# S5 prompt recurrence: a walk over chunk pairs, and a scan in levels in two halves

## The chip, the core and the metric

The kernel runs on one core of one Trainium2 chip. PE (TensorE) multiplies matrices, DVE (VectorE), ACT (ScalarE) and POOL (GpSimd) work on vectors, and SP issues most of the transfers. The metric is the device time of one execution in microseconds; lower is better. The profile is one execution of the same program, taken by the hardware profiler; its lines are explained where they are shown.

## The reference, cut to what matters

One layer of a decoder in float32: a prompt of 256 tokens and 8 samples of 4 tokens each. Two groups of heads run side by side on one input projection; the second, S5, is a diagonal complex recurrence over time.

```python
D_MODEL = 2048; SEQ = 256; DEC_BATCH = 8; DEC_SEQ = 4
S5_CH = 16; S5_GROUPS = 64; S5_STATE = 64

def s5_scan(u, lam_re, lam_im, log_step, b_re, b_im, c_re, c_im, d_skip, h0_re, h0_im):
    ...
    lam_bar = jnp.exp(lam * dt)
    ...
    bu = jnp.einsum('gpk,blgk->blgp', b_bar, uf.astype(jnp.complex64))
    h0 = lax.complex(h0_re.astype(f32), h0_im.astype(f32))
    bu = bu.at[:, 0].add(lam_bar * h0)
    a = jnp.broadcast_to(lam_bar, bu.shape)
    def combine(e1, e2):
        a1, b1 = e1
        a2, b2 = e2
        return a1 * a2, a2 * b1 + b2
    _, h = lax.associative_scan(combine, (a, bu), axis=1)
    y = jnp.real(jnp.einsum('gkp,blgp->blgk', cmat, h)) + d_skip.astype(f32) * uf
    h_last = h[:, -1]
    return y, jnp.real(h_last), jnp.imag(h_last)

def layer(x, c, gla_s, s5_re, s5_im, conv_s, w):
    ...
    h = modulate(rmsnorm(x, w['norm1']), sh1, sc1)
    proj = jnp.einsum('bld,de->ble', h, w['w_in'])
    q, k, v, g, a_lr, u = jnp.split(proj, cuts, axis=-1)
    ...
    o, gla_new = gla_chunked(q, k, v, log_a, gla_s)
    ...
    y5, re_new, im_new = s5_scan(u.reshape(bsz, l, S5_GROUPS, S5_CH), ...)
    ...
```

The layer goes on with a gated output projection, a convolution over three tokens and a feed-forward part; these are not touched.

## The kernel before

**Tiles and stages.** Every weight comes from HBM once, as tiles `raw` of 128x1024. ACT (line 126) makes the high part `wh` of one, DVE (line 128) the rest `wl`, and PE runs three matmuls for each block of 128 rows (lines 143 to 145: `wh` with the high part of the input, `wh` with its low part, `wl` with the high part). All 288 tokens, 32 of the samples and 256 of the prompt, lie side by side, so such a matmul is 128x288. Between the projections stand groups of matmuls of the condition vector (line 191, `ada`), which use a `raw` without a split.

**S5.** Four tokens make a chunk. The prompt has 64 chunks and the samples one each, so the state `st` has per partition 2 (real, imaginary) x 32 blocks of two channel groups x 73 columns: 8 for the samples' start states, one of zeros, 64 for the chunks. For each of the 8 projections f of u (lines 653 to 684), PE finishes the projection and transposes it twice (lines 663 and 669, with the tiles `us` and, copied by ACT, `vt`), and multiplies with the input matrices (line 679); ACT copies the result into four blocks of `st` and into `deci`, the samples' part (lines 680 and 681). A complex product of a coefficient and a state is done as two multiplies and two adds over both parts, the second with the parts swapped. `advance` (line 647) does that with `a4`, the transition over one chunk: after each f it adds every even chunk (0, 2, ...) to the odd one behind it, on POOL, for f=7 on DVE. With all eight f done, the samples' end state is made on DVE (lines 686 to 690) and written out by a transfer that POOL issues (line 691, `o_s5d`).

**The walk.** Then, on POOL, the loop of line 692 goes over the chunk pairs: 31 steps, each of which takes the state two chunks back, multiplies it with `a8` (the transition over two chunks) and adds it to the present one, for all 32 blocks at once, 128x64:

```python
for c in range(3, NC4, 2):
    ...
    G.tensor_tensor(q1, prev, a8[:, 0], op=ALU.mult)
    G.tensor_tensor(q2, prevs, a8[:, 1], op=ALU.mult)
    G.tensor_tensor(cur, cur, q1, op=ALU.add)
    G.tensor_tensor(cur, cur, q2, op=ALU.add)
```

The last column is the prompt's end state (line 703). Later, for each f (lines 841 to 868), `advance` fills the chunks between (31 columns, on DVE for even f, on POOL for odd), PE makes the outputs (line 853 from the input, line 855 from `st` with `cA`), ACT copies them to `zt`, and PE transposes back.

**What else runs there.** Projections m=8 to 15 (lines 707 to 713), the attention matrix of the other group in levels of 32, 16, 8, 4, 2 and 1 tokens (lines 763 to 781: two differences and two products on DVE, an exponential on ACT, then matmuls in line 738 or 752), its states (lines 785 to 833), and projections m=16 to 23 (lines 835 to 838). The first level's tile takes the slot `S11` that `deci` had, so it waits until `o_s5d` is read out.

**What sets the order.** Each engine works through its own list. A scheduler makes the lists from the program's order and its own estimate of durations; a rank far ahead is given only to the loading and splitting of weights (`high_priority`, lines 105, 114, 124), and the ada groups are kept in one piece (`chained`, line 165). The ring `t2k` has three buffers of 128x512 (line 236), which `vt`, `zt`, `dt1` and the products `q` of `advance` share in the order in which the program names them.

Of the kernel before, what the change touches and what calls it, by code (L numbers as in the profile page):

```python
# [12 lines left out]
F32 = mybir.dt.float32  # L13
# [3 lines left out]
ALU = mybir.AluOpType  # L17
# [3 lines left out]
P = 128  # L21
# [35 lines left out]
def tile_hybrid_step(ctx: ExitStack, tc: _tile.TileContext, a: dict):  # L57
# [15 lines left out]
    def nm(s):  # L73
        cnt[0] += 1
        return f"{s}_{cnt[0]}"
# [159 lines left out]
    with ExitStack() as early:  # L235
# [83 lines left out]
        V.tensor_sub(w1, w1, w2)  # L319
        V.tensor_mul(fi, w1, den)  # L320

        def bc16(x):
            return x.unsqueeze(2).to_broadcast([P, 32, 16])

# [296 lines left out]
        for h in range(H):  # L621
# [9 lines left out]
            V.tensor_sub(l2, l2, l1)  # L631
            V.tensor_tensor_scan(cum[:, h], cst[:, C_RST:C_RST + NT], l2, 0.0, op0=ALU.mult, op1=ALU.add)


        a4 = epb.tile([P, 2, 2, 32], F32, name="a4")
        a8 = epb.tile([P, 2, 2, 32], F32, name="a8")
        for t in (a4, a8):
            if t is a4:
                V.tensor_copy(t[:, 0, 0], AP[:, 3, 0])
                V.tensor_copy(t[:, 1, 1], AP[:, 3, 1])  # L640
            else:
                cmul(t[:, 0, 0], t[:, 1, 1], AP[:, 3, 0], AP[:, 3, 1], AP[:, 3, 0], AP[:, 3, 1],
                     t[:, 0, 1], t[:, 1, 0])
            V.tensor_copy(t[:, 0, 1], t[:, 0, 0])
            V.tensor_scalar_mul(t[:, 1, 0], t[:, 1, 1], -1.0)

        def advance(eng, dst, src, srcs, fs, n):
            for w_, x in ((0, src), (1, srcs)):
                q = t2k.tile([P, 512], F32, tag="t2k", name=nm("q"))[:, 0:8 * n].rearrange(
                    "p (r a c) -> p r a c", r=2, a=4)  # L650
                eng.tensor_tensor(q, x, a4[:, w_, :, fs].unsqueeze(3).to_broadcast([P, 2, 4, n]), op=ALU.mult)
                eng.tensor_tensor(dst, dst, q, op=ALU.add)

        ut = []
        for f in range(8):
            m = f
            ps = proj2(f)
            us = sml.tile([P, 4, NCOL], F32, tag="us", name=nm("us"))
            V.tensor_tensor(us, ps.rearrange("p (c s) -> p s c", s=4), pu[f].rearrange("p (c s) -> p s c", s=4),
                            op=ALU.add)  # L660
            pvv = ps_s5()
            for s in range(4):
                T.transpose(pvv[0:NCOL, s * P:(s + 1) * P], us[:, s], ident)
            vt = t2k.tile([P, 512], F32, tag="t2k", name=nm("vt"))
            S.copy(vt[0:NCOL].rearrange("p (g s k) -> p s g k", g=8, s=4),
                   pvv[0:NCOL].rearrange("p (s g k) -> p s g k", s=4, g=8))
            puu = ps_s5()
            for aj in range(4):
                T.transpose(puu[:, aj * NCOL:(aj + 1) * NCOL], vt[0:NCOL, aj * P:(aj + 1) * P], ident[0:NCOL, 0:NCOL])
            u_f = slot(f"UU{f}", [P, 4, NCOL])  # L670
            S.copy(u_f, puu[:, 0:4 * NCOL].rearrange("p (a c) -> p a c", a=4))
            ut.append(u_f)
            for r in range(2):
                pi = ps_gl()[:, 0:4 * NCOL].rearrange("p (a c) -> p a c", a=4)
                for al_ in range(4):
                    pr = 4 * f + al_
                    for j in range(2):
                        js = slice(64 * j, 64 * j + 64)
                        T.matmul(pi[js, al_], pt_t[pr // 16][r][js, pr % 16], u_f[js, al_], start=True, stop=True)
                S.copy(st[:, r, 4 * f:4 * f + 4, NB + 1:], pi[:, :, NB:])  # L680
                S.copy(deci[:, r, 4 * f:4 * f + 4], pi[:, :, 0:NB])
            fs = slice(4 * f, 4 * f + 4)
            advance(V if f == 7 else G, st[:, :, fs, NB + 2::2], st[:, :, fs, NB + 1::2], st[:, ::-1, fs, NB + 1::2], fs, 32)
            step(ada_b, 1)

        dt1 = t2k.tile([P, 512], F32, tag="t2k", name="dt1").rearrange("p (r a b) -> p r a b", r=2, a=32)
        for w_, src in ((0, st[:, :, :, 0:NB]), (1, st[:, ::-1, :, 0:NB])):
            for r in range(2):
                V.tensor_tensor(dt1[:, r], src[:, r], a4[:, w_, r].unsqueeze(2).to_broadcast([P, 32, NB]), op=ALU.mult)
            V.tensor_add(deci, deci, dt1)  # L690
        G.dma_start(a["o_s5d"], deci)
        for c in range(3, NC4, 2):
            prev = st[:, :, :, NB + c - 1]
            prevs = st[:, ::-1, :, NB + c - 1]
            cur = st[:, :, :, NB + c + 1]
            q1 = sml.tile([P, 2, 32], F32, tag="q1", bufs=1, name=nm("q1"))
            q2 = sml.tile([P, 2, 32], F32, tag="q2", bufs=1, name=nm("q2"))
            G.tensor_tensor(q1, prev, a8[:, 0], op=ALU.mult)  # L698
            G.tensor_tensor(q2, prevs, a8[:, 1], op=ALU.mult)  # L699
            G.tensor_tensor(cur, cur, q1, op=ALU.add)  # L700
            G.tensor_tensor(cur, cur, q2, op=ALU.add)  # L701
        s5p = epb.tile([P, 2, 32], F32, name="s5p")
        G.tensor_copy(s5p, st[:, :, :, NCOL])
        G.dma_start(a["o_s5p"], s5p)
# [135 lines left out]
        ybuf = []  # L840
        for f in range(8):
            fs = slice(4 * f, 4 * f + 4)
            advance(G if f % 2 else V, st[:, :, fs, NB + 3::2], st[:, :, fs, NB + 2:NCOL:2], st[:, ::-1, fs, NB + 2:NCOL:2],
                    fs, 31)
            zt = t2k.tile([P, 512], F32, tag="t2k", name=nm("zt"))
            ztv = zt[0:NCOL].rearrange("p (t a j k) -> p a j t k", t=4, a=4, j=2)
            pzs = [ps_s5()[0:NCOL, 0:256], ps_s5()[0:NCOL, 0:256]]
            for al_ in range(4):
                pr = 4 * f + al_
                for j in range(2):  # L850
                    js = slice(64 * j, 64 * j + 64)
                    o = pzs[j][:, al_ * 64:(al_ + 1) * 64]
                    T.matmul(o, ut[f][js, al_], mm_[js, pr], start=True, stop=False)  # L853
                    for r in range(2):
                        T.matmul(o, st[js, r, pr, 0:NCOL], cA[js, r, pr].rearrange("p t k -> p (t k)"),  # L855
                                 start=False, stop=(r == 1))
            for j in range(2):
                S.copy(ztv[:, :, j], pzs[j].rearrange("p (a t k) -> p a t k", a=4, t=4))
            py = ps_tr()
            for t_ in range(4):  # L860
                T.transpose(py[:, t_ * NCOL:(t_ + 1) * NCOL], zt[0:NCOL, t_ * P:(t_ + 1) * P], ident[0:NCOL, 0:NCOL])
            yb = slot(f"UU{f}", [P, NT])
            V.tensor_copy(yb.rearrange("p (c s) -> p s c", s=4),
                          py[:, 0:4 * NCOL].rearrange("p (s c) -> p s c", s=4))
            ybuf.append(yb)
            ps = proj2(24 + f)
            V.tensor_add(proj_dst(24 + f), ps, proj_dst(24 + f))
            step(ada_b, 1)
# [469 lines left out]
```

## Time and profile before

| | us |
|---|---|
| three runs | 1486.63, 1487.9, 1977.88 |
| their median | 1487.9 |
| the profiled execution | 1486.31 |
| its span in the profile | 1484.0 |
| mean granted clock of PE | 0.982 of full speed |

The span goes from the first to the last recorded instruction; some 2.3 us of the execution lie around it. The third run stands far above the other two, and the profiled execution is near the lower ones. Busy time of an engine is the sum of its instructions; matmuls overlap, so their number times their mean is more than PE's busy time.

### The profile page before, as it was taken

The numbers are of one execution on the slowest core, as the hardware profiler recorded it, in microseconds if no ns is written. First come the engines' busy times: TensorE is split into PE (matmuls) and PEld (weight loads), VectorE is DVE, ScalarE is ACT, GpSimd is POOL, SyncE is SP. The second block draws the span as 40 slices with busy tenths as digits, with TensorE's granted clock in tenths as the row PEclk, the third lists the DMA queues.
The fourth block names the chain that finished last, engine by engine and source line by source line (L and its number), as shares of the span: only waits on it lengthen the run. The fifth ranks groups of instructions, "written<-read, shape, count | busy, mean of one in ns | idle before, by whom it ended". The sixth has DMA issues, their size and how long they took to land.

```text
span 1484.0 us, 28963 instructions
## 1 busy us (share of the span) xinstructions
PE 1412.4 (95%) x11534; PEld 1301.3 (88%) x11534; DVE 903.6 (61%) x1646; ACT 681.2 (46%) x1142; POOL 347.9 (23%) x622
## 2 busy tenths in 40 slices
PE   4998999985999999899999999999999999999996
PEld 3877877874777898688999999999999999999995
DVE  7774673582366777755665666555656565566557
ACT  4741354333353446454435543454345534553445
POOL 1163013496211001322202220222023201330121
PEclk9999999997999999999999999999999999999998
DMA  9778978881689686678444435444544444445432
GB/s 374 278 287 233 383 278 287 282 299 70 241 286 335 244 311 234 248 265 289 168 175 170 163 141 191 161 170 157 171 169 159 171 160 167 166 161 170 147 104 79
DMA packets 88727, 316.95 MB, mean 214 GB/s; under 512 B 10368, under 2 KB 10784, under 8 KB 88592
## 3 DMA queue, kind: packets, MB, share of 16 engines
q1 hardware_dynamic: 84240, 299.72, 56.6%
q0 software_dynamic: 4064, 14.81, 2.9%
q8 instruction: 90, 1.47, 0.4%
q10 hardware_dynamic: 288, 0.59, 0.1%
q14 instruction: 45, 0.37, 0.1%
HBM read 306.63 MB, written 8.45 MB: 212 GB/s over the span
## 4 chain that ended last, share of the span: by engine, by line
PE 73%; POOL 4%; DVE 2%; DMA 1%; ACT 1%; issue 1%; DVEq 0%; SPq 0%; ACTq 0%; POOLq 0%
PE acc L143 22%; PE acc L145 22%; PE acc L144 22%; PE ada L191 3%; POOL q L699 1%; POOL st L701 1%; POOL q L698 1%; POOL st L700 1%; PE gl L918 1%; DMA raw<-wup 1%; PE s L855 1%; PE s L853 0%; DVE S L1071 0%; PE acc L1122 0%; PE gl L895 0%
## 5 line engine op out<-in xcount | busy, mean ns | idle before, releaser
L126 ACT CAST wh<-raw 128x1024 fp32r<-128x1024 f32 (+1 forms) x376 | 385.9, 1030 | 565.0 <-PE acc L144 486.4
L128 DVE TENSOR_TENSOR wl<-raw,wh 128x1024 fp32r<-128x1024 f32 (+1 forms) x376 | 454.6, 1211 | 297.6 <-ACT wh L126 287.3
L143 PE MATMUL acc<-hh,wh 128*128 128x288 f32 x1376 | 407.7, 296 | 0.0
L144 PE MATMUL acc<-hl,wh 128*128 128x288 f32 x1376 | 405.9, 295 | 0.0
L145 PE MATMUL acc<-hh,wl 128*128 128x288 f32 x1376 | 404.5, 294 | 0.0
L143 PEld LDWEIGHTS acc<-hh,wh 128*128 128x128 f32 x1376 | 257.8, 187 | 4.2 <-ACT up L1132 4.2
L145 PEld LDWEIGHTS acc<-hh,wl 128*128 128x128 f32 x1376 | 259.1, 188 | 0.0
L144 PEld LDWEIGHTS acc<-hl,wh 128*128 128x128 f32 x1376 | 258.3, 188 | 0.0
L1133 POOL COPY cvo<-up 128x16 f32<-128x16 f32 x88 | 101.7, 1156 | 595.5 <-ACT up L1131 595.5
L144 PE MATMUL acc<-ffhl,wh 128*128 128x288 f32 x704 | 208.1, 296 | 0.0
L145 PE MATMUL acc<-ffhl,wl 128*128 128x288 f32 x704 | 207.6, 295 | 0.0
L143 PE MATMUL acc<-ffhl,wh 128*128 128x288 f32 x704 | 207.1, 296 | 0.5 <-ACT ffhl L1163 0.2
L143 PE MATMUL acc<-h,wh 128*128 128x288 f32 x512 | 158.6, 311 | 4.3 <-ACT h L477 3.1
L145 PE MATMUL acc<-h,wl 128*128 128x288 f32 x512 | 153.7, 301 | 1.3 <-DVE wl L128 1.3
L144 PE MATMUL acc<-h,wh 128*128 128x288 f32 x512 | 153.7, 300 | 1.0 <-DVE h L478 1.0
L144 PEld LDWEIGHTS acc<-ffhl,wh 128*128 128x128 f32 x704 | 132.7, 188 | 0.1
L143 PEld LDWEIGHTS acc<-ffhl,wh 128*128 128x128 f32 x704 | 131.9, 188 | 0.9 <-ACT ffhl L1163 0.5
L145 PEld LDWEIGHTS acc<-ffhl,wl 128*128 128x128 f32 x704 | 132.0, 188 | 0.0
L1009 DVE SCALAR_TENSOR_TENSOR x<-acc,mod,x 128x256 f32<-128x256 f32 x128 | 61.6, 481 | 98.0 <-PE acc L145 97.7
L143 PEld LDWEIGHTS acc<-h,wh 128*128 128x128 f32 x512 | 97.7, 191 | 26.8 <-issue 9.4
L191 PE MATMUL ada<-raw,cS 128*32 128x512 f32 (+1 forms) x832 | 101.0, 574 | 5.8 <-DMA raw<-wadf 4.1
L145 PEld LDWEIGHTS acc<-h,wl 128*128 128x128 f32 x512 | 97.8, 191 | 2.0 <-DVE wl L128 1.5
(413 smaller groups left out, 1978.1 us busy)
## 6 DMA issues: line engine op xcount, KB each, us to landing
raw<-wup SPq DMA_DIRECT2D x176, 512.0 KB, 3.4
raw<-wadf SPq DMA_DIRECT2D x128, 512.0 KB, 6.1
raw<-wdn SPq DMA_DIRECT2D x80, 512.0 KB, 3.4
raw<-wadb SPq DMA_DIRECT2D x48, 512.0 KB, 7.8
raw<-win SPq DMA_DIRECT2D x32, 512.0 KB, 6.6
raw<-winc SPq DMA_DIRECT2D x32, 512.0 KB, 5.5
raw<-wout SPq DMA_DIRECT2D x32, 512.0 KB, 7.3
raw<-wad SPq DMA_DIRECT2D x16, 512.0 KB, 8.9
```

What stands on the lines that cost most here:

```text
L126: S.copy(wh, raw)
L128: V.tensor_sub(wl, raw, wh.bitcast(F32))
L143: T.matmul(ps, wh[:, ks], xh(k), start=first, stop=False)
L144: T.matmul(ps, wh[:, ks], xl(k), start=False, stop=False)
L145: tail[0] = T.matmul(ps, wl[:, ks], xh(k), start=False, stop=last).ins
L191: mms.append(lambda c=c, kc=kc_of(blk, j), raw=raw, c0=c0, first=first, last=last: T.matmul(ps[32 * c:32 * c + 32, 0:w], cS[:, kc, :], raw ...
L698: G.tensor_tensor(q1, prev, a8[:, 0], op=ALU.mult)
L699: G.tensor_tensor(q2, prevs, a8[:, 1], op=ALU.mult)
L700: G.tensor_tensor(cur, cur, q1, op=ALU.add)
L701: G.tensor_tensor(cur, cur, q2, op=ALU.add)
L1009: V.scalar_tensor_tensor(x2[:, m, ND:], ps[:, ND:], mod[:, vi, m, 0:1], x2[:, m, ND:], op0=ALU.mult, op1=ALU.add)
L1133: G.tensor_copy(cvo[:, m, 0:16].rearrange("p (b w) -> p b w", w=2), upd[:, :, 4:6])
```

## The change

The walk is replaced by `scan`, which works on 16 blocks at a time: after f=3 on blocks 0 to 15, after f=7 on blocks 16 to 31, both on POOL. After `advance` of level 0 (chunk pairs) it goes up: at level 1 every fourth chunk takes in the one two before it, at level 2 every eighth the one four before it, at level 3 every sixteenth the one eight before it. Then three steps one behind another carry the state over 16 chunks (level 4), and levels 3, 2 and 1 go down and fill the odd chunks between. Each advance is four instructions as before, so a half has 9 advances and 36 instructions, and the walk's 124 are gone. The coefficients are now powers of the transition over 1, 2, 4, 8 and 16 chunks (`apr`, `api`), made by DVE at the start of S5; `a4` and `a8` go. The products `q` of the scan come from the ring `t2k`, where the walk had its own `q1` and `q2`. The level-0 advances and those ahead of the outputs do the same arithmetic with the new tables.

```diff
--- before.py
+++ after.py
@@ -318,6 +318,21 @@
         V.tensor_mul(w2, w3, lam_i)
         V.tensor_sub(w1, w1, w2)
         V.tensor_mul(fi, w1, den)
+
+
+        apr = epb.tile([P, 5, 32], F32, name="apr")
+        api = epb.tile([P, 5, 2, 32], F32, name="api")
+        for i in range(5):
+            if i == 0:
+                V.tensor_copy(apr[:, 0], AP[:, 3, 0])
+                V.tensor_copy(api[:, 0, 1], AP[:, 3, 1])
+            else:
+                s_r, s_i = apr[:, i - 1], api[:, i - 1, 1]
+                cmul(apr[:, i], api[:, i, 1], s_r, s_i, s_r, s_i, w1, w2)
+            V.tensor_scalar_mul(api[:, i, 0], api[:, i, 1], -1.0)
+
+        def trans(w_, lev, fs):
+            return apr[:, lev, fs].unsqueeze(1).to_broadcast([P, 2, fs.stop - fs.start]) if w_ == 0 else api[:, lev, :, fs]
 
         def bc16(x):
             return x.unsqueeze(2).to_broadcast([P, 32, 16])
@@ -631,25 +646,29 @@
             V.tensor_sub(l2, l2, l1)
             V.tensor_tensor_scan(cum[:, h], cst[:, C_RST:C_RST + NT], l2, 0.0, op0=ALU.mult, op1=ALU.add)
 
-
-        a4 = epb.tile([P, 2, 2, 32], F32, name="a4")
-        a8 = epb.tile([P, 2, 2, 32], F32, name="a8")
-        for t in (a4, a8):
-            if t is a4:
-                V.tensor_copy(t[:, 0, 0], AP[:, 3, 0])
-                V.tensor_copy(t[:, 1, 1], AP[:, 3, 1])
-            else:
-                cmul(t[:, 0, 0], t[:, 1, 1], AP[:, 3, 0], AP[:, 3, 1], AP[:, 3, 0], AP[:, 3, 1],
-                     t[:, 0, 1], t[:, 1, 0])
-            V.tensor_copy(t[:, 0, 1], t[:, 0, 0])
-            V.tensor_scalar_mul(t[:, 1, 0], t[:, 1, 1], -1.0)
-
-        def advance(eng, dst, src, srcs, fs, n):
-            for w_, x in ((0, src), (1, srcs)):
-                q = t2k.tile([P, 512], F32, tag="t2k", name=nm("q"))[:, 0:8 * n].rearrange(
-                    "p (r a c) -> p r a c", r=2, a=4)
-                eng.tensor_tensor(q, x, a4[:, w_, :, fs].unsqueeze(3).to_broadcast([P, 2, 4, n]), op=ALU.mult)
+        def advance(eng, fs, lev, c0, dist, n):
+
+            na, back = fs.stop - fs.start, 1 << lev
+
+            def cols(rs, c):
+                return st[:, rs, fs, NB + 1 + c:NB + 2 + c + dist * (n - 1):dist]
+
+            dst = cols(slice(None), c0)
+            for w_, rs in ((0, slice(None)), (1, slice(None, None, -1))):
+                q = t2k.tile([P, 512], F32, tag="t2k", name=nm("q"))[:, 0:2 * na * n].rearrange(
+                    "p (r a c) -> p r a c", r=2, a=na)
+                eng.tensor_tensor(q, cols(rs, c0 - back), trans(w_, lev, fs).unsqueeze(3).to_broadcast([P, 2, na, n]),
+                                  op=ALU.mult)
                 eng.tensor_tensor(dst, dst, q, op=ALU.add)
+
+        def scan(eng, fs):
+
+            for lev in (1, 2, 3):
+                advance(eng, fs, lev, (2 << lev) - 1, 2 << lev, NC4 >> (lev + 1))
+            for c in range(31, NC4, 16):
+                advance(eng, fs, 4, c, 1, 1)
+            for lev in (3, 2, 1):
+                advance(eng, fs, lev, (3 << lev) - 1, 2 << lev, (NC4 >> (lev + 1)) - 1)
 
         ut = []
         for f in range(8):
@@ -680,25 +699,17 @@
                 S.copy(st[:, r, 4 * f:4 * f + 4, NB + 1:], pi[:, :, NB:])
                 S.copy(deci[:, r, 4 * f:4 * f + 4], pi[:, :, 0:NB])
             fs = slice(4 * f, 4 * f + 4)
-            advance(V if f == 7 else G, st[:, :, fs, NB + 2::2], st[:, :, fs, NB + 1::2], st[:, ::-1, fs, NB + 1::2], fs, 32)
+            advance(V if f == 7 else G, fs, 0, 1, 2, NC4 // 2)
+            if f % 4 == 3:
+                scan(G, slice(4 * f - 12, 4 * f + 4))
             step(ada_b, 1)
 
         dt1 = t2k.tile([P, 512], F32, tag="t2k", name="dt1").rearrange("p (r a b) -> p r a b", r=2, a=32)
         for w_, src in ((0, st[:, :, :, 0:NB]), (1, st[:, ::-1, :, 0:NB])):
             for r in range(2):
-                V.tensor_tensor(dt1[:, r], src[:, r], a4[:, w_, r].unsqueeze(2).to_broadcast([P, 32, NB]), op=ALU.mult)
+                V.tensor_tensor(dt1[:, r], src[:, r], (apr[:, 0] if w_ == 0 else api[:, 0, r]).unsqueeze(2).to_broadcast([P, 32, NB]), op=ALU.mult)
             V.tensor_add(deci, deci, dt1)
         G.dma_start(a["o_s5d"], deci)
-        for c in range(3, NC4, 2):
-            prev = st[:, :, :, NB + c - 1]
-            prevs = st[:, ::-1, :, NB + c - 1]
-            cur = st[:, :, :, NB + c + 1]
-            q1 = sml.tile([P, 2, 32], F32, tag="q1", bufs=1, name=nm("q1"))
-            q2 = sml.tile([P, 2, 32], F32, tag="q2", bufs=1, name=nm("q2"))
-            G.tensor_tensor(q1, prev, a8[:, 0], op=ALU.mult)
-            G.tensor_tensor(q2, prevs, a8[:, 1], op=ALU.mult)
-            G.tensor_tensor(cur, cur, q1, op=ALU.add)
-            G.tensor_tensor(cur, cur, q2, op=ALU.add)
         s5p = epb.tile([P, 2, 32], F32, name="s5p")
         G.tensor_copy(s5p, st[:, :, :, NCOL])
         G.dma_start(a["o_s5p"], s5p)
@@ -840,8 +851,7 @@
         ybuf = []
         for f in range(8):
             fs = slice(4 * f, 4 * f + 4)
-            advance(G if f % 2 else V, st[:, :, fs, NB + 3::2], st[:, :, fs, NB + 2:NCOL:2], st[:, ::-1, fs, NB + 2:NCOL:2],
-                    fs, 31)
+            advance(G if f % 2 else V, fs, 0, 2, 2, NC4 // 2 - 1)
             zt = t2k.tile([P, 512], F32, tag="t2k", name=nm("zt"))
             ztv = zt[0:NCOL].rearrange("p (t a j k) -> p a j t k", t=4, a=4, j=2)
             pzs = [ps_s5()[0:NCOL, 0:256], ps_s5()[0:NCOL, 0:256]]
```

The scheduler makes new lists from this. Line numbers of the changed file lie some 11 to 19 higher: 688 was 669, 682 was 663, 698 was 679, 865 was 855, 763 was 752, 749 was 738, 712 was 691, and the four lines of `advance` are now 660 and 662.

First PE at the S5 inputs of f=4, where the list before has the transposes of `vt` for f=4 (line 669) and of `us` for f=5 (line 663) behind m=8 and an ada group, in the first matmuls of m=9:

```order
L191 MATMUL ada_2419<-raw_3238,cS 32x512 x2
L143 MATMUL acc_3258<-h_1800,wh_3254 128x288
L144 MATMUL acc_3258<-h_1800,wh_3254 128x288
L669 MATMUL s_455_2717<-ident,vt_2715 128x72 x4
L663 MATMUL s_469_2799<-ident,us_2797 72x128 x4
L145 MATMUL acc_3258<-h_1800,wl_3256 128x288
```

and now the same two (lines 688 and 682), in the last part of m=14:

```order
L143 MATMUL acc_3393<-h_1833,wh_3389 128x288
L144 MATMUL acc_3393<-h_1833,wh_3389 128x288
L688 MATMUL s_473_2790<-ident,vt_2788 128x72 x4
L682 MATMUL s_487_2872<-ident,us_2870 72x128 x4
L145 MATMUL acc_3393<-h_1833,wl_3391 128x288
```

What moved: between f=3's line 679 and these two transposes the list before has 24 matmuls of a projection and one ada group, the new one 162 matmuls and three groups, since m=9 to 14 went ahead of f=4. (`s` are PSUM tiles of S5, `acc` of projections.)

Next POOL at the transfer `o_s5d`, early in the walk before, between the third and fourth instruction of one of its first steps:

```order
L698 TENSOR_TENSOR q_513_3033<-st,a_2329 128x64
L699 TENSOR_TENSOR q_514_3034<-st,a_2329 128x64
L700 TENSOR_TENSOR st<-st,q_513_3033 128x64
L691 DMA o_s5d<-S_371_2264 128x512
L701 TENSOR_TENSOR st<-st,q_514_3034 128x64
L698 TENSOR_TENSOR q_515_3039<-st,a_2329 128x64
```

and now at the end of the second scan, after the levels (`q` products with `apr` or `api`, the last number the columns of one block):

```order
L662 TENSOR_TENSOR st<-st,q_3122 128x2x16x7
L662 TENSOR_TENSOR st<-st,q_3125 128x2x16x7
L660 TENSOR_TENSOR q_3128<-st,apr 128x480
L660 TENSOR_TENSOR q_3131<-st,api 128x480
L662 TENSOR_TENSOR st<-st,q_3128 128x2x16x15
L712 DMA o_s5d<-S_371_2297 128x512
L662 TENSOR_TENSOR st<-st,q_3131 128x2x16x15
L660 TENSOR_TENSOR q_4228<-st,apr 128x248
```

What moved: the transfer went from a place some 30 instructions into the walk to the place before the last instruction of the second scan.

Last PE at the outputs of f=0. Before, line 855 stands behind all levels of the attention matrix and the transposes of v (line 879):

```order
L879 MATMUL gl_4875<-ident,PV_26_319 128x128 x4
L879 MATMUL gl_4881<-ident,PV_27_320 128x128 x4
L879 MATMUL gl_4887<-ident,PV_26_319 32x128 x4
L855 MATMUL s_695_4202<-cA,st 72x64 x2
L855 MATMUL s_696_4203<-cA,st 72x64 x2
L853 MATMUL s_695_4202<-MM_1323,UU_395_2389 72x64
```

and now line 865 is done ahead of the coarse level (line 763), which reads the tile `S` in the slot of `deci`:

```order
L863 MATMUL s_669_4143<-MM_1356,UU_395_2408 72x64
L865 MATMUL s_669_4143<-cA,st 72x64 x2
L863 MATMUL s_670_4144<-MM_1356,UU_395_2408 72x64
L865 MATMUL s_670_4144<-cA,st 72x64 x2
L763 MATMUL gl_3522<-S_596_3516 32x32 x16
L749 MATMUL gl_3549<-S_598_3543 32x32 x32
L871 MATMUL tr_4171<-ident,zt_4142 128x72 x4
L143 MATMUL acc_4186<-h_1833,wh_4182 128x288
```

What moved: the outputs of f=0 come before the attention levels, not behind them.

## The prediction

> **What bounds the kernel now.** I read the page first: how busy PE is, then the chain that ended last.
>
> ```profile
> span 1484.0 us, 28963 instructions
> PE 1412.4 (95%) x11534; PEld 1301.3 (88%) x11534; DVE 903.6 (61%) x1646; ACT 681.2 (46%) x1142; POOL 347.9 (23%) x622
> PE 73%; POOL 4%; DVE 2%; DMA 1%; ACT 1%; issue 1%; DVEq 0%; SPq 0%; ACTq 0%; POOLq 0%
> ```
>
> PE works 95% of the span, so only its idle time can be won. POOL is busy for 23% but holds 4% of the chain, and lines 698 to 701, the walk, make up that share. Next the waits of PE, and the timeline at both ends of the walk (start, duration, engine, line; in brackets the idle time before and who ended it):
>
> ```profile
> PE s L855 <- DVE st L652: 13.8, 1, 13.8
> ```
>
> ```profile
> 287.14 0.36 POOL L698 TENSOR_TENSOR q<-st,a 128x64 f32<-128x64 f32 x1 [3.06 <-DVE st L652]
> 287.45 4.59 POOL L699 TENSOR_TENSOR q<-st,a 128x64 f32<-128x64 f32 x1
> ...
> 348.45 0.35 POOL L698 TENSOR_TENSOR q<-st,a 128x64 f32<-128x64 f32 x1
> ...
> 349.93 0.35 POOL L698 TENSOR_TENSOR q<-st,a 128x64 f32<-128x64 f32 x1
> ...
> 352.44 0.35 POOL L701 TENSOR_TENSOR st<-st,q 128x64 f32<-128x64 f32 x1
> 352.82 0.90 DVE L651 TENSOR_TENSOR q<-st,a 128x248 f32<-128x248 f32 x2 [15.99 <-POOL st L701]
> ...
> 354.82 0.75 PE L855 MATMUL s<-cA,st 64*72 64x64 f32 x8 [13.84 <-DVE st L652]
> ```
>
> The walk runs from 287.1 to 352.8, 65.7 us; PE runs out of other work 13.84 us before L855 may start. With DVE idle a step takes 349.93-348.45 = 1.48 us, so 31 steps would take 45.7; the other 20 us go where DVE is busy too, as in the 4.59 us of one L699. The windows (busy us of PE, PEld, DVE, ACT and POOL, PE's clock, DMA) show it by stretch:
>
> ```profile
> 244.00:260.00 16.00, 16.00 (x148) 12.50 (x148) 6.55 (x8) 6.85 (x14) 7.32 (x9) 1.00 0.81 291
> 260.00:272.00 12.00, 12.00 (x112) 9.19 (x110) 6.00 (x6) 3.91 (x9) 5.42 (x6) 1.00 0.61 222
> ...
> 287.00:300.00 13.00, 13.00 (x161) 10.92 (x154) 8.54 (x14) 2.51 (x3) 12.15 (x20) 1.00 0.84 306
> 300.00:310.00 10.00, 8.43 (x143) 6.16 (x144) 5.62 (x8) 3.23 (x4) 9.21 (x21) 1.00 1.00 371
> 310.00:320.00 10.00, 8.49 (x209) 6.56 (x197) 10.00 (x15) 3.79 (x7) 9.45 (x14) 1.00 0.79 270
> 320.00:330.00 10.00, 9.96 (x216) 7.91 (x216) 10.00 (x16) 4.11 (x4) 9.53 (x13) 1.00 0.58 211
> 330.00:340.00 10.00, 7.16 (x52) 6.07 (x48) 4.09 (x8) 7.22 (x17) 9.14 (x23) 0.83 0.63 239
> 340.00:352.80 12.80, 0.98 (x8) 0.54 (x7) 0.00 (x0) 2.71 (x6) 11.46 (x35) 0.60 0.00 1
> 352.80:370.00 17.20, 15.18 (x155) 12.08 (x156) 7.03 (x13) 6.96 (x14) 6.04 (x11) 0.80 0.21 76
> ```
>
> PE has no idle time from 244 to 300. From 300 to 370 its idle time adds up to 1.57+1.51+0.04+2.84+11.82+2.02 = 19.8 us. That, and a few us at a clock of 0.60 to 0.83, is all that the change can win: some 22 us, 1.5%. DVE was busy 38.3 us between 287 and 340 and POOL lost 20, so POOL loses about 0.52 us per busy us of DVE.
>
> **Price of a scan half.** The walk's 124 POOL instructions go. Two scans of 36 come, each on 16 blocks; by the diff their instructions have 512, 256, 128, three times 32, 96, 224 and 480 elements, four instructions for each size: 1792 elements, twice multiplied and twice added. Rows of one line (count: minimum/median/maximum ns):
>
> ```profile
> L399 POOL TENSOR_TENSOR t<-s_s,AP x4: 1057/1148/1566, 54.1 to 106.9; 128x512 f32<-128x512 f32 x4
> L405 POOL TENSOR_TENSOR cA<-t,t x4: 1262/1378/2281, 90.5 to 116.7; 128x512 f32<-128x512 f32 x4
> L651 POOL TENSOR_TENSOR q<-st,a x22: 599/630/1256, 217.0 to 403.9; 128x256 f32<-128x256 f32 x14, 128x248 f32<-128x248 f32 x8
> L652 POOL TENSOR_TENSOR st<-st,q x22: 720/752/1752, 218.9 to 409.3; 128x256 f32<-128x256 f32 x14, 128x248 f32<-128x248 f32 x8
> L698 POOL TENSOR_TENSOR q<-st,a x31: 345/352/1308, 287.1 to 352.9; 128x64 f32<-128x64 f32 x31
> L700 POOL TENSOR_TENSOR st<-st,q x31: 346/357/1346, 292.0 to 353.9; 128x64 f32<-128x64 f32 x31
> ```
>
> A multiply with a repeated coefficient goes from 599 (256) to 1057 (512): 141 ns and 1.79 per element; an add from 720 to 1262: 178 and 2.12. By these a half takes 18x0.141+3.584x1.79 + 18x0.178+3.584x2.12 = 19.8, with gaps of 0.02 about 20.4 us. The walk's rows, which step over a whole row of the state, lie above that line: (345-141)/64 = 3.19 and (346-178)/64 = 2.63 ns per element, which makes 27.2. I take 24, midway: the scan steps through the state as the walk did, but its coefficient is repeated as in L651. All up to the last advance is then 18.7 us.
>
> The Trainium skill speaks against the change here (GPSIMD Engine Reference, section 7, Performance pitfalls for Q7 kernels): reads that step by more than 8 bytes cost about 2.9 cycles an element in place of 1.9. L651's step is 8 bytes and the walk's larger, and L698 lies 35% over L651's line, so the trace leans to the rule; with half as much again on all elements a half would take some 27 us and the sum come to about 1497, inside the forecast's own range below.
>
> **Scan 1 (f=3) and its cover.** It starts where f=3's advance ends, and no PE matmul before that moves:
>
> ```profile
> 246.54 1.58 POOL L652 TENSOR_TENSOR st<-st,q 128x256 f32<-128x256 f32 x2
> ```
>
> That is 248.1. Its tiles come from a ring of three buffers (t2k) shared with f=4's vt, whose copy on ACT now waits for all but the last advance. DVE is busy 12.55 of 28 us here, so POOL is slowed by 0.52x0.45 = 0.23: (18.7+0.5 for the two qbd copies)/0.77 = 25, that is 273.1, and 0.6 for the copy. Queued behind vt are f=4's transposes on PE. They now stand after 162 projection matmuls and three ada groups, at prices of these rows:
>
> ```profile
> 220.49 0.42 PE L669 MATMUL s<-ident,vt 72*128 72x72 f32 x4
> ...
> 221.10 0.38 PE L144 MATMUL acc<-h,wh 128*128 128x288 f32 x1
> ...
> 224.91 1.22 PE L679 MATMUL gl<-UU,PT 64*64 64x72 f32 x32
> 226.06 1.92 PE L191 MATMUL ada<-raw,cS 128*32 128x512 f32 x14
> 227.91 0.40 PE L143 MATMUL acc<-h,wh 128*128 128x288 f32 x1
> 228.15 0.30 PE L144 MATMUL acc<-h,wh 128*128 128x288 f32 x1
> ...
> 230.01 0.29 PE L143 MATMUL acc<-h,wh 128*128 128x288 f32 x1
> ```
>
> From 228.15 to 230.01 are 14 matmuls: 0.133 each. An ada group has 16 records: 14 take 1.85, all 2.1. So 243.9+162x0.133+3x2.1 = 271.7, and PE waits about 2 us for vt, where it waited for nothing; if scan 1 is quick, 0. From there to the end of f=7's L679 stand 129 matmuls, three groups, four units of 0.7 and 1.15 and a transpose: 31.5 us, so that end, P7, is 305.2.
>
> **Scan 2 and f=0's outputs.** After P7 the copies and f=7's advance on DVE take 2.3. DVE has about four L128 and four PSUM adds beside the scan (some 7 us in 22), a slowing of 0.17: 18.7/0.83 = 22.5, so R, the end of all but the last advance, is P7+24.8. Then DVE's dt1 and f=0's odd columns, which share the ring, need the last advance: 5.9 more, P7+30.7. PE reaches f=0's L855 after 91 matmuls, two groups and a level of attention, 17.7 us after P7. Wait: 13.0, against 13.84. The walk's stall is not removed, since scan 2 is still a chain of 24 us after the last input, and of the projections m=16 to 23 that filled PE beside the walk, four now stand among f=4 to 7, since m=8 to 14 are spent beside scan 1.
>
> **The moved DMA.** o_s5d is now issued behind the scan's last multiply; the DVE operation that writes the same slot waits for it:
>
> ```profile
> 297.85 0.59 POOL L691 DMA_DIRECT2D o_s5d<-S  x1
> ...
> 304.38 0.81 DVE L771 TENSOR_TENSOR S<-S 128x512 f32<-128x512 f32 x1 [5.47 <-DMA o_s5d<-S]
> 305.12 0.84 DVE L772 TENSOR_TENSOR S<-S 128x512 f32<-128x512 f32 x1
> ...
> 305.99 1.06 ACT L773 ACTIVATE S<-S 128x1024 f32<-128x1024 f32 x1 [4.70 <-DVE S L772]
> ```
>
> 6.5 us from issue to L771; before, PE had projections meanwhile. Now issue is at about R+3.6, L771 at R+10.1, and two more DVE steps after ACT's put the coarse attention matmuls at R+13.9. PE is done with f=0's outputs (some 3 us at the low clock, an estimate) at R+8.9: a new wait of 5. The levels behind it, five at four DVE steps and an exponential each, leave PE another 3 (0 to 5, an estimate from the four steps of 0.8 and 1.06 of ACT).
>
> **Startup.** The powers add 19 small DVE instructions; such rows are:
>
> ```profile
> L300 DVE TENSOR_TENSOR a<-a 128x32 f32<-128x32 f32 x1 | 0.2, 186 | 0.0
> ...
> 60.06 1.23 DVE L128 TENSOR_TENSOR wl<-raw,wh 128x1024 fp32r<-128x1024 f32 x1 [2.64 <-ACT wh L126]
> ```
>
> At most 19x0.186 = 3.5 us of DVE, with 2.64 us idle ahead of 60; on the path between 0 and 2, taken 0.5, since DVE is nearly full there.
>
> **Sum.** Idle after: 2+13+5+3 = 23; before 19.8; +3.2, and 0.5 of startup: +3.7. The profiled execution took 1486.3, so 1490.0; the median of the runs, 1487.9, lies 1.6 higher. I forecast 1491.
>
> **Rivals.** (A) Faster: POOL runs at the low price, undisturbed, and the attention levels find other work for PE. To the last advance a half is then 16 us: wait at scan 1 none, at L855 2.3+16+5-17.7 = 5.6, with 5 and 0 to 5 behind: 10.6 to 15.6 in place of 19.8, that is 1478 to 1484, and 1474 if the DMA costs nothing. For it: L652 at 720 ns already steps through the state. Against: DVE's weight splits (L128) never pause.
> (B) Slower: POOL is held by DVE as in the walk (45.7/65.7 = 0.70) and pays the high price, 21 us to the last advance. Each half takes 30: 6.5 of wait at scan 1, 2.3+30+8-17.7 = 22.6 at L855, 7 and 5 behind it: 41 against 19.8, about 1509. It decides against the change once the two halves together cost over 5 us more than I take. For it: the 4.59 us L699; against: DVE is at 45%, not 72%, beside scan 1.
> (C) The scan does what it says and the stall goes whole: 1486.3-22 = 1466. For that scan 2 must be done 13 us earlier, in some 10 us; 36 instructions at the rows' fixed cost and elements exclude it almost.
>
> **How the numbers follow.** My forecast 0.55, its own range 1484 to 1498; A 0.24; B 0.14; C 0.02; the rest, 0.05, on either side. Range 1476 to 1509: it leaves out the far ends of A, B and C. About 2% (29.8 us) is what a measurement of this kernel can tell from no change: faster needs 1458 or less, below the 22 us there are, 0.02; slower needs 1518, beyond B, 0.05; within, 0.93.
>
> **What would show it.** Scan 1 on POOL from 248 to about 280, with PE waiting 0 to 5 us at f=4's transposes; an L855 wait of about 13; then a new wait at the coarse attention matmuls with DVE idle on o_s5d. Instructions of 512 elements in a scan at 1.1 us speak for A, at 1.8 for B. I am wrong if L855 no longer waits, or if PE stalls again between f=4 and f=7.

## The result, and the profile after

| kernel | median us | runs (lowest to highest) | ratio to before, 95% interval |
|---|---|---|---|
| before | 1487.27 | 1485.03 to 1977.88 | |
| changed | 1512.64 | 1508.95 to 1515.22 | 1.0179 [1.0164, 1.0195] |

The run of 1977.88 stands far above the other runs of the same kernel and is left out of the ratio. Without it the median before is 1486.63, so the change costs 26.0 us, 1.8%. I forecast 1491 and a range of 1476 to 1509; the time lies above it. The page of the changed kernel's profile (its execution took 1511.78):

```profile
span 1510.0 us, 28933 instructions
...
PE 1422.6 (94%) x11534; PEld 1311.6 (87%) x11534; DVE 914.9 (61%) x1665; ACT 684.1 (45%) x1144; POOL 340.8 (23%) x570
...
PE 83%; DVE 7%; POOL 3%; DMA 3%; ACT 2%; issue 1%; SPq 0%; DVEq 0%; ACTq 0%; POOLq 0%
```

PE's idle time grew from 1484.0-1412.4 = 71.6 to 87.4 us, +15.8. Its busy time grew as well, by 10.2 us for the same number of matmuls, and the mean granted clock fell from 0.982 to 0.972. Both together are the 26 us of the span. The waits of PE (waiting engine and line, releaser, us in total, times, longest):

```profile
PE s L865 <- DVE st L662: 17.4, 1, 17.4
...
PE acc L143 <- ACT mixo L1011: 5.6, 1, 5.6
PE s L396 <- DVE pn L380: 5.1, 1, 5.1
PE acc L143 <- DVE PK L602: 4.3, 2, 4.0
...
PE gl L749 <- DVE S L786: 3.1, 1, 3.1
...
PE s L688 <- ACT vt L684: 2.5, 1, 2.5
```

The wait before f=0's outputs is there still, 17.4 us against 13.84. The one for the levels (line 749) was 1.5 before, and the other four are new or were 0.2 at most. Three of these lie at places of which the prediction says nothing: the transposes of `pn` (line 396), at 50 us, `PK` (line 602), at about 100, and `mixo` (line 1011), behind 500 us. (The larger waits left out of the list stand in the kernel before as well.)

Where did the time go? First to the start. POOL clears a tile as soon as PE has done f=3's input matmuls, so this row tells when these end:

```profile
252.50 0.95 POOL L730 MEMSET PT<- 128x1024 f32 x1 [5.94 <-PE gl L698]
```

Before, the same row stands at 244.01: 8.5 us are lost ahead of any scan. The windows of before and after (busy us of PE, PEld, DVE, ACT and POOL, then PE's clock, the share of the DMA engines, GB/s) show the place; first before:

```profile
40.00:50.00 10.00, 9.10 (x65) 8.40 (x64) 9.63 (x20) 7.68 (x18) 0.00 (x0) 1.00 0.91 339
50.00:60.00 10.00, 10.00 (x98) 8.90 (x96) 7.35 (x13) 7.27 (x17) 4.56 (x3) 1.00 0.73 260
```

and after:

```profile
40.00:50.00 10.00, 6.80 (x46) 5.89 (x45) 10.00 (x32) 4.89 (x12) 0.00 (x0) 1.00 0.88 340
50.00:60.00 10.00, 7.34 (x50) 6.53 (x54) 6.61 (x16) 5.30 (x13) 3.83 (x3) 0.66 0.03 11
```

PE does nothing from 47.6 to 52.7 us and ACT nothing from 45.7 to 53.8. From 50 to 60 the transfers of weights nearly stop (DMA share 0.03), and PE's clock is 0.66. The timelines of ACT and PE there say what each waited for (the bracket names the idle time before an instruction):

```profile
45.28 0.40 ACT L598 ACTIVATE PQ<-acc 128x288 f32<-128x288 f32 x1
53.78 0.31 ACT L398 COPY PT<-s 64x192 f32<-64x192 f32 x1 [8.10 <-PE s L396]
54.10 0.37 ACT L401 COPY PT<-s 64x256 f32<-64x256 f32 x1
54.49 1.01 ACT L598 ACTIVATE PK<-acc 128x288 f32<-128x288 f32 x3
...
52.66 2.98 PE L396 MATMUL s<-ident,pn 128*128 128x128 f32 x12 [5.06 <-DVE pn L380]
```

The first copy of a K projection out of PSUM into `PK` is made at 54.49; before, that copy stood at 46.94. And these are the last of the powers on DVE:

```profile
52.74 0.21 DVE L301 TENSOR_TENSOR PK<-apr,api 128x32 f32<-128x32 f32 x1
52.84 0.21 DVE L302 TENSOR_TENSOR PK<-api,apr 128x32 f32<-128x32 f32 x1
52.94 0.71 DVE L383 TENSOR_TENSOR t<-s_s,AP 128x512 f32<-128x512 f32 x1
53.54 0.21 DVE L303 TENSOR_TENSOR api<-PK 128x32 f32<-128x32 f32 x1
```

They write their products into `PK`: `w1` and `w2`, the scratch of `cmul`, lie in the slot that the K projections take over. That copy cannot start until the last product is read at 53.7. Ahead of it the scheduler's lists now have the transposes of `pn`, which PE and ACT must do before they go on with the projections, and for `pn` PE waits in this trace. DVE, which makes `pn` beside the powers, is busy all the time from 40 to 50 us. That the shared slot brought this order about is a reading so far; the third round of experiments tests it.

Then the scans, and what stands behind the second. On POOL the first runs from 256.68, the second from 318.94; with the start of the last advance of each:

```profile
256.68 2.23 POOL L660 TENSOR_TENSOR q<-st,apr 128x512 f32<-128x512 f32 x1
258.87 1.29 POOL L660 TENSOR_TENSOR q<-st,api 128x512 f32<-128x512 f32 x1
...
282.23 1.23 POOL L660 TENSOR_TENSOR q<-st,apr 128x480 f32<-128x480 f32 x1
...
318.94 1.33 POOL L660 TENSOR_TENSOR q<-st,apr 128x512 f32<-128x512 f32 x1 [1.92 <-DVE st L662]
...
334.29 0.27 POOL L660 TENSOR_TENSOR q<-st,apr 128x32 f32<-128x32 f32 x1
...
342.81 1.44 POOL L660 TENSOR_TENSOR q<-st,apr 128x480 f32<-128x480 f32 x1
```

25.5 and 23.9 us up to the last advance. On DVE and PE behind it:

```profile
342.76 1.77 DVE L710 TENSOR_TENSOR dt<-st,apr 128x256 f32<-128x256 f32 x2 [5.96 <-POOL st L662]
...
348.83 0.42 DVE L660 TENSOR_TENSOR q<-st,apr 128x248 f32<-128x248 f32 x1
349.28 0.42 DVE L662 TENSOR_TENSOR st<-st,q 128x248 f32<-128x248 f32 x1
349.61 2.09 DVE L660 TENSOR_TENSOR q<-st,api 128x248 f32<-128x248 f32 x1
351.74 0.42 DVE L662 TENSOR_TENSOR st<-st,q 128x248 f32<-128x248 f32 x1
352.07 0.69 DVE L782 TENSOR_TENSOR S<-S 128x512 f32<-128x512 f32 x1
```

```profile
352.30 0.75 PE L865 MATMUL s<-cA,st 64*72 64x64 f32 x8 [17.44 <-DVE st L662]
356.33 0.66 PE L763 MATMUL gl<-S 128*32 128x32 f32 x32 [0.86 <-DVE S L786]
```

The samples' end state (lines 710 and 711) starts only at 342.76, takes six us beside POOL's last advance, and stands ahead of f=0's odd columns. The attention levels start at 352.07, where the first (line 771) stood at 304.38 before. Much later that returns. The other group's prompt state can be written out only when the levels and the transposes of v are through, and the samples' states of that group pass through its buffers, each with a transfer in and one out from POOL. Before, the first and the last of these transfers out:

```profile
377.30 0.53 POOL L897 DMA_DIRECT2D o_glap<-S  x1
...
485.33 0.53 POOL L938 DMA_DIRECT2D o_glad<-MM  x1 [4.07 <-DVE MM L936]
```

and after:

```profile
427.61 0.54 POOL L907 DMA_DIRECT2D o_glap<-S  x1 [0.97 <-ACT PV L991]
...
524.28 0.54 POOL L948 DMA_DIRECT2D o_glad<-MM  x1 [2.28 <-DVE MM L946]
```

The last is 39 us later, and with them the inputs `mixo` of the output projection. Their last cast on ACT, before and after:

```profile
528.06 1.15 ACT L1001 CAST mixo<-PV 128x1152 fp32r<-128x1152 f32 x1
...
559.40 1.15 ACT L1011 CAST mixo<-PV 128x1152 fp32r<-128x1152 f32 x1 [6.13 <-DVE PV L1010]
```

PE, which had run ahead with what else there was, waits 5.6 us for it. When PE does f=7's outputs, the changed kernel is only 7.9 us late (423.7 against 415.8), less than the 8.5 of the start. But more of the other group's states is still to be done: the matmuls on the samples' states (line 928, 918 before) run from 436 to 519 us, where they ran from 385 to 477. From f=7's outputs to the first convolution tile PE is idle for 15.4 us in place of 8.5 and busy for 11 us more; there the changed kernel is 25.7 us late (650.8 against 625.1).

### The profile page after: what moved, and what is told of

Read it like the earlier page. It is cut to its first block, busy times and chain, and to the rows that moved or that the text cites. A ratio compares the mean times of both kernels' runs of the same rounds, so it can differ in the third digit from the quotient of the medians.

```text
span 1510.0 us, 28933 instructions
## 1 busy us (share of the span) xinstructions
PE 1422.6 (94%) x11534; PEld 1311.6 (87%) x11534; DVE 914.9 (61%) x1665; ACT 684.1 (45%) x1144; POOL 340.8 (23%) x570
## 4 chain that ended last, share of the span: by engine, by line
PE 83%; DVE 7%; POOL 3%; DMA 3%; ACT 2%; issue 1%; SPq 0%; DVEq 0%; ACTq 0%; POOLq 0%
PE acc L143 24%; PE acc L144 24%; PE acc L145 24%; PE ada L191 5%; POOL st L662 2%; POOL q L660 2%; DVE wl L128 1%; PE gl L928 1%; DMA raw<-wadb 1%; DMA o_glap<-S 1%; PE s L396 1%; DMA raw<-wup 1%; ACT wh L126 1%; PE gl L698 1%; DMA S<-xT 0%
## 5 line engine op out<-in xcount | busy, mean ns | idle before, releaser
L143 PE MATMUL acc<-h,wh 128*128 128x288 f32 x512 | 162.2, 318 | 7.8 <-DVE PK L602 4.3
L144 PE MATMUL acc<-h,wh 128*128 128x288 f32 x512 | 156.2, 305 | 0.8 <-DVE h L493 0.8
L143 PEld LDWEIGHTS acc<-h,wh 128*128 128x128 f32 x512 | 100.6, 197 | 29.6 <-issue 11.1
L144 PEld LDWEIGHTS acc<-h,wh 128*128 128x128 f32 x512 | 100.9, 197 | 2.2 <-DVE h L493 1.2
```

The lines of the kernel that those rows point to most:

```text
L143: T.matmul(ps, wh[:, ks], xh(k), start=first, stop=False)
L144: T.matmul(ps, wh[:, ks], xl(k), start=False, stop=False)
```

## The experiments

**First: the start, and the order behind the scan.** Theory 1 puts 8.5 us on the tables of powers; theory 2 puts the other 17 on the end state and its transfer, which were left behind the scan. Four kernels, in three rounds each beside the one before (1485.93). The changed kernel did not run again in these rounds or the later ones. The one before gave 1486.63, 1485.93, 1484.9 and 1485.11 from round to round, so a difference to the change's 1512.64 is sure to some 2 us only.

The tables without the scan:

```diff
-            if f % 4 == 3:
-                scan(G, slice(4 * f - 12, 4 * f + 4))
...
+        for c in range(3, NC4, 2):
+            ...
+            G.tensor_tensor(q1, prev, apr[:, 1].unsqueeze(1).to_broadcast([P, 2, 32]), op=ALU.mult)
+            G.tensor_tensor(q2, prevs, api[:, 1], op=ALU.mult)
+            G.tensor_tensor(cur, cur, q1, op=ALU.add)
+            G.tensor_tensor(cur, cur, q2, op=ALU.add)
```

> The changed kernel with its power tables, but with the walk of before in place of the two scans (the walk takes its products from the ring t2k). Theory 1: the 19 added small DVE instructions at the start, and the transposes of pn that they bring forward on PE, cost 8.5 us by themselves: f=3's inputs end at about 252 instead of 244, and the time is about 1496. Rival: the tables cost nothing (0 to 1 us, as I predicted) and the 8.5 us belong to something else in the change: about 1487 to 1488.

Measured: 1497.29, 1.008 [1.0065, 1.0095], +11.4 us. f=3's inputs end still later than in the change, at 253.6:

```profile
253.64 0.95 POOL L738 MEMSET PT<- 128x1024 f32 x1 [5.96 <-PE gl L698]
```

The tables cost 11 us without any scan; the rival falls. PE's waits for `pn` (5.1 us) and `PK` (4.3) are the same as in the change.

The tables on POOL:

```diff
-                cmul(apr[:, i], api[:, i, 1], s_r, s_i, s_r, s_i, w1, w2)
-            V.tensor_scalar_mul(api[:, i, 0], api[:, i, 1], -1.0)
+                g_ = api[:, i, 0]
+                G.tensor_mul(apr[:, i], s_r, s_r)
+                G.tensor_mul(g_, s_i, s_i)
+                G.tensor_sub(apr[:, i], apr[:, i], g_)
+                G.tensor_mul(g_, s_r, s_i)
+                G.tensor_add(api[:, i, 1], g_, g_)
+            G.tensor_scalar_mul(api[:, i, 0], api[:, i, 1], -1.0)
```

> The changed kernel with the power tables made by POOL, which is idle until 54 us, in place of DVE; the scans stay. Theory 1: the start goes back to that of before (f=3's inputs end at about 244), the rest keeps its cost: about 1504. Rival (the start is not due to the tables on DVE): about 1512, f=3 at 252.

Measured: 1499.85, 1.0094 [1.0077, 1.0111], 12.8 us under the change. f=3's inputs end at 241.2, earlier than before the change:

```profile
241.16 0.95 POOL L734 MEMSET PT<- 128x1024 f32 x1 [5.96 <-PE gl L702]
```

POOL has nothing else to do there: in the change it stands from 5.4 to 52.9 us. The move costs nothing at the start, and DVE is rid even of the twelve small instructions that the kernel before had.

The end state ahead of the second scan:

```diff
+            if f == 7:
+                dt1 = t2k.tile([P, 512], F32, tag="t2k", name="dt1").rearrange("p (r a b) -> p r a b", r=2, a=32)
+                ...
+                G.dma_start(a["o_s5d"], deci)
             if f % 4 == 3:
                 scan(G, slice(4 * f - 12, 4 * f + 4))
...
-        dt1 = t2k.tile([P, 512], F32, tag="t2k", name="dt1").rearrange("p (r a b) -> p r a b", r=2, a=32)
-        ...
-        G.dma_start(a["o_s5d"], deci)
```

> The changed kernel with the samples' end state (dt1, deci) and its transfer o_s5d written ahead of the second scan instead of behind it; the scan is the same. Theory 2: some 17 us of the loss come from the attention levels, which had to wait for o_s5d and moved behind f=0's outputs, and with them the states of the other group (POOL's transfers ended at 524 instead of 485) and the wait for mixo of 5.6 us: about 1498, and the last transfer of those states before 495. Rival 2: the loss after the start is the wait at line 865 for the scan, 17.4 us, and stays: 1509 to 1513.

Measured: 1496.53, 1.0077 [1.0062, 1.0092], 16.1 us under the change. In its profile the transfer and the end of the other group's states (POOL) read:

```profile
324.99 0.59 POOL L709 DMA_DIRECT2D o_s5d<-S  x1
...
407.86 0.53 POOL L908 DMA_DIRECT2D o_glap<-S  x1
...
493.06 0.53 POOL L949 DMA_DIRECT2D o_glad<-MM  x1 [3.14 <-DVE x L1025]
```

The transfer is issued at 325.0 and not at 349.4, the levels run beside the scan, and the states are through 31 us sooner. The wait for f=0's outputs is still 11.8 us, yet nearly all of the 17 us are back: rival 2 falls as the main cause. Nor is it the shorter wait that gives them. PE does f=7's outputs at 425.8, where the change did them at 423.7; the gain is made behind them, where no wait for `mixo` is left, and the first convolution tile comes at 635.8 and not at 650.8.

The second scan on DVE:

```diff
-                scan(G, slice(4 * f - 12, 4 * f + 4))
+                scan(V if f == 7 else G, slice(4 * f - 12, 4 * f + 4))
```

> The changed kernel with the second scan on DVE in place of POOL, where its 36 instructions should take some 13 us instead of 31. Rival 2 (the loss is the length of the second scan): the wait at line 865 falls from 17.4 to about 5 us and the time to about 1498. Theory 2 (the loss is the order of what comes behind): the wait falls as well, but the levels still stand behind f=0's outputs: 1503 to 1510.

Measured: 1506.3, 1.0142 [1.0127, 1.0157]; PE waits 11.0 us for f=0's outputs. A shorter scan (18.0 us to its last advance in place of 23.9) gives 6.3 us, less than half of what the order gives, as theory 2 had it. The wait for `mixo` stays, 5.5 us.

**Second: the parts together, and what the scan itself brings.** Five rounds each beside the one before (1484.9). The edits are those above, put together: tables on POOL and end state ahead of the second scan; then the second scan on DVE as well.

> Tables on POOL and the samples' end state ahead of the second scan, both at once; the two scans stay as in the change. Theories 1 and 2 together, if their parts add: 1512.6-12.8-16.1 = 1484, so no slower than before. Rival: both parts give back the same idle time, and it stays at 1490 to 1496.

Measured: 1483.5, 0.9993 [0.9984, 1.0003]. The two parts add: 1512.64-12.8-16.1 = 1483.7. With tables and end state moved, the change costs nothing any more.

> As pool_deci, and the second scan on DVE. If the wait for the scan at line 865 (11.8 us left with the end state ahead) still sets the time: another 6 to 8 us off, 1476 to 1478. Rival: DVE, which also makes the attention levels, becomes what PE waits for there, and it stays at 1484 or more.

Measured: 1482.53, 0.9987 [0.9979, 0.9995], the fastest kernel of the study and by its interval just faster than before. The time lies between what I expected and the rival's 1484, but the mechanism is the rival's: PE's wait moved from the outputs to the levels. The waits of this kernel:

```profile
PE gl L754 <- DVE S L791: 7.0, 2, 6.5
PE gl L754 <- DVE st L666: 5.7, 1, 5.7
```

Both scans behind f=7:

```diff
-            if f % 4 == 3:
-                scan(G, slice(4 * f - 12, 4 * f + 4))
+            if f == 7:
+                scan(G, slice(0, 16))
+                scan(G, slice(16, 32))
```

> As pool_deci, but both scans behind f=7, so that no half is done early. If the early half is what the scan brings: the wait at line 865 grows by some 10 us or more and the time is 1492 to 1500. Rival: the early half only moves the wait (the projections it hides behind are missing later), and the time is 1482 to 1488.

Measured: 1485.17, 1.0005 [0.9996, 1.0013]. The early half is worth some 1.7 us, and the intervals overlap. The rival holds: the wait for f=0's outputs did not grow by 10 us but fell from 11.8 to 2.9, and PE waits more for the levels (8.1 us) and the weight splits (4.1) instead.

The walk (as in the first experiment) with the tables on POOL (as in the second):

> The walk of before with the tables on POOL: the change without its scan and without its cost at the start. f=3's inputs end at 241 to 242; the time is about 1483, some 3 us under before. If the scan itself is worth something, pool_deci is faster than this by more than the intervals; if the scan only moves the wait, the two agree within 2 us.

Measured: 1484.66, 1.0001 [0.9992, 1.001], and f=3's inputs end at 241.4. That is 12.6 us under walk_new_tables, so the tables cost the walk what they cost the scan. The interval overlaps that of pool_deci: on equal terms scan and walk take the same time, to about 1 us.

**Third: why the tables cost that much, and one try to shorten the scan.** Five rounds each (before: 1485.11).

The same 31 instructions on DVE with other scratch:

```diff
-                cmul(apr[:, i], api[:, i, 1], s_r, s_i, s_r, s_i, w1, w2)
+                cmul(apr[:, i], api[:, i, 1], s_r, s_i, s_r, s_i, api[:, i, 0], api[:, i, 1])
```

> The change with the same 31 small DVE instructions for the tables, whose four products per power go to the tables' own spare parts instead of w1 and w2. These two lie in the slot PK, which the projections of K take over next, so in the change ACT's copy of K out of PSUM could start only after the last power, at 54.5 us. Theory 1a: that wait, and PE's order that was made around it, is the cost at the start, not DVE's time: f=3's inputs end near 244, and the time is about 1500, as with the tables on POOL. Rival 1b: DVE's time for 19 more instructions is the cost: 1508 to 1513.

Measured: 1503.63, 1.012 [1.0099, 1.0141], 9.0 us under the change and 3.8 over the tables on POOL. f=3's inputs end at 243.3, and ACT's first copy into `PK` is back at 46.8:

```profile
243.31 0.95 POOL L730 MEMSET PT<- 128x1024 f32 x1 [5.96 <-PE gl L698]
```

```profile
46.82 0.41 ACT L598 ACTIVATE PK<-acc 128x288 f32<-128x288 f32 x1
```

The waits for `pn` and `PK` are gone, as they are from every profile of this study without the shared scratch (`PK` 0.2 us at most), while all four with it have both. So of the 12.8 us that the tables on POOL give back, about nine are the shared scratch, with the order that came of it. The rest, about four, goes with the work on DVE, but it is less sure: the intervals of tables_own and tables_pool overlap, and at the first convolution tile the two are 0.8 us apart (641.0 and 640.2). Theory 1a holds for the larger part.

That scratch with the end state ahead of the second scan, and the second scan on DVE:

> As pool_deci_dve (end state ahead of the second scan, second scan on DVE), but with the tables on DVE with their own scratch. Theory 1a: within 3 us of pool_deci_dve, that is 1481 to 1486. Rival 1b: 1490 or more.

Measured: 1486.76, 1.0012 [1.0, 1.0024], 4.2 us over pool_deci_dve, and here the intervals do not meet: some four us again, a little outside what I expected of theory 1a. Whether DVE's time costs them or the order that the scheduler made with it, no run separates.

The second scan on both engines at once:

```diff
+        def scan(parts):
+            ...
+            def both(*a_):
+                for (eng, fs), qt in zip(parts, qts):
+                    advance(eng, fs, *a_, qt=qt)
...
+                scan([(G, slice(0, 16))] if f == 3 else [(V, slice(16, 24)), (G, slice(24, 32))])
```

> As pool_deci, but the second scan has 8 of its 16 blocks on DVE and 8 on POOL, level by level side by side, each with one tile for its products. If the two engines ran it side by side, it would take some 14 us instead of 28 on POOL, PE's wait of 11.8 us at line 870 would mostly go, and the time would be about 1475. Rival: they hold each other up, and with what DVE has to do besides the time stays at 1481 to 1486.

Measured: 1489.07, 1.0023 [1.0012, 1.0034], slower than either engine alone, and outside both forecasts. POOL's half of the blocks takes from 306.68 to 333.6, 27 us, where all 16 blocks took 35.8 in pool_deci. DVE's half, with splits and levels between, ends only at 342.0, so the whole scan takes 35.6 us, as on POOL alone; first, middle and last rows of POOL's half:

```profile
306.68 0.93 POOL L665 TENSOR_TENSOR qs<-st,apr 128x256 f32<-128x256 f32 x1 [3.06 <-DVE st L667]
...
316.95 2.05 POOL L667 TENSOR_TENSOR st<-st,qs 128x64 f32<-128x64 f32 x2
...
331.10 2.52 POOL L667 TENSOR_TENSOR st<-st,qs 128x240 f32<-128x240 f32 x2
```

Two adds of 64 elements take 2.05 us, where one such add of the walk took 0.35: POOL is held up beside DVE. That is not the whole loss, since PE also waits 9.5 us for `zt`, a tile of the ring from which the split takes two of three buffers, and 4.3 for `mixo`; the parts were not separated.

## Why the prediction was wrong, step by step

- **The gain of 22 us at most, and "the stall is not removed":** right. The wait for f=0's outputs stayed, 17.4 us, and with the other costs taken away scan and walk come out alike (1483.5 and 1484.66).
- **Price of a half, 24 us undisturbed:** right: the fastest rows of each size in the two scans add up to about 24 us. Multiplies of 512 elements took 1.29 and 1.33 us, of 32 elements 0.27, that is 2.1 to 2.2 ns per element, between my ends of 1.79 and 3.19. The rule of the Trainium skill that I weighed (GPSIMD Engine Reference, section 7) would have put half as much again on 1.79, 2.7. The trace shows some 20% (27% at 256 elements, 0.76 us against line 651's 0.60 before), so here the measurement decides against the full 50%.
- **Scan 1:** right. 25.5 us to the last advance (forecast 25.0), and 2.5 us of wait for `vt` (forecast 2).
- **Scan 2:** its length was right, 23.9 (22.5). Behind it the term "5.9 more" was mis-sized: from the last advance to PE's start passed 9.5 us, since DVE's end state took 6.0 us and one product of f=0 2.09 instead of 0.42, with POOL at work beside them. So the wait was 17.4 and not 13.0.
- **The moved DMA:** wrong in size, and in what it costs. DVE started the first level 2.7 us after the issue, not 6.5, and PE waited 0.86 for the coarse level, not 5. The other levels made PE wait 3.1, as forecast. The price was the place of the levels, 48 us later in the program's time, which the sum put at nothing.
- **Startup, taken 0.5 of 0 to 2:** this term failed first, and by most in proportion: 8.5 us at f=3's end, 11.4 to 12.8 in the whole time by the runs. I counted the durations of 19 small instructions and looked at how full DVE was. I did not ask whose memory the scratch was: `w1` and `w2` stand in `PK`, the powers keep that slot until 53.7, and the copies of the K projections had to come behind it. PE's order shows it too: 208 matmuls stand ahead of the first transposes of `pn`, where 276 did. The working left out the lists ahead of f=0.
- **The sum:** the ledger ended at f=0's outputs and the levels and took the rest as equal. In truth the levels, part of the transposes of v and the first work on the other group's states had filled PE beside the walk. Moved behind the scan, they came back as `mixo` late, PE waiting from 555 to 560.6 us, and matmuls at a lower clock behind that (0.91 from 540 to 580 us, 1.00 before). Some 60% of the loss, 16 of 26 us by the run with the end state ahead, lie in this step.
- **Rival B** came out near the time (1509), but for another reason: POOL was not held up as it said, and both scans took what I forecast.

## What to carry to other kernels

Shorter chains on an engine that is not the bound are worth nothing until the wait that they end is shown to shrink; here two scans of known price replaced a walk at the same time to a microsecond. Look at an edit's side products before its main one: the tables, with scratch that shares a slot with the next stage, and a small output left behind a long chain cost 12.8 and 16.1 us, where the chain itself cost nothing. When work is moved ahead of a stall, follow what it displaced to the place where that is needed next, even if it is 200 us away.

## What the runs showed of the hardware

- DVE and POOL can slow each other in both directions. POOL's second scan took 29.5 us to its last advance in deci_first, with DVE busy for 20.9 of them, and 23.9 in the change, with DVE busy for 7.8. DVE's multiply of 248 elements took 2.09 us beside POOL's add, and 0.42 just before, while POOL stood; each pair of multiplies of line 710 took 1.77 and 1.88 us beside POOL, where a pair of line 689 took 0.75 before. DVE does not always lose: the second pair of line 689 took 0.75 too, beside POOL's multiply of 4.59. The Trainium skill (GPSIMD Engine Reference, section 1, Specifications) says that POOL shares its ways to SBUF with DVE, with contention from DVE instructions of two SBUF inputs; the trace agrees, and shows that DVE loses as well.
- A scan split over both engines, with DVE's other work between, took as long as on POOL alone (35.6 and 35.8 us).
- Waits cost more than their length here. Behind the wait of 5.1 us for `pn`, projection matmuls started 0.24 us apart (55.67 to 57.59) and then 0.13 again, and the granted clock from 50 to 60 us was 0.66. Over the whole kernel PE's busy time for as many matmuls grew by 10.2 us, with the mean granted clock at 0.972 in place of 0.982.
